# Sparse attention of a two-layer decoder: the compressed keys' weights for both row blocks in one pass, another layout and other PSUM banks for the first products, and a new order of steps

## The chip, the cores and the metric

The kernel runs on one core of one Trainium2 chip. The metric is the device time of one execution in microseconds (us): the median over runs, and for the profile one execution of its own. A core has five engines with a queue each: TensorE (PE, whose weight loads are shown as PEld), VectorE (DVE), ScalarE (ACT), GpSimd (POOL) and SyncE (SP, which here only issues DMAs). An engine takes its instructions in the order of the program; it waits where an operand isn't ready, and what stands behind waits with it.

## What is computed

A trunk of two layers on x of 256 rows by 1024 columns, in float32: each layer is a SwiGLU feed-forward part, a mixer, another feed-forward part, with a layer norm behind each. The second layer's mixer is native sparse attention (NSA), and the change lies in it alone. Cut to what matters:

```python
q, k_c, v_c, k_s, v_s, k_w, v_w, g = split(x @ w_in)     # 16 heads of 64 in 4 groups; 4 key/value heads
q, k_s, k_w = rope(q), rope(k_s), rope(k_w)
gates = sigmoid(g)                                       # three per head
def compress(t, pe, w1, w2):                             # 15 blocks of 32 rows, 16 apart
    blk = concatenate([ch[:, :-1], ch[:, 1:]], axis=2) + pe   # ch: t cut into pieces of 16 rows
    return gelu(blk . w1) @ w2
k_cmp, v_cmp = rope(compress(k_c, ...)), compress(v_c, ...)
p_cmp = masked_softmax(q . k_cmp);  o_cmp = p_cmp . v_cmp
o_slc, o_win = softmax attention with k_s, v_s and with k_w, v_w   # 256 rows: every block is chosen
out = (g0 * o_cmp + g1 * o_slc + g2 * o_win) @ w_out
```

## The kernel before

The 256 rows are two row blocks, T = 0 and 1, of 128 rows, one row per partition. A product with a weight matrix is three matmuls (`mm3`): the weights are cut into a high part `whi` (a rounded copy, ACT, L221) and a low part `wlo` (the rest, DVE, L222), and so are the activations. Weights come in pieces of up to 128x1024 by DMA into four `raw` buffers; a ring of eight split pieces (`RING`) runs ahead of PE, and a piece's place comes free when PE has used it for T = 1. The order in which the weights lie and stream is that of the steps.

`nsa` is written as steps, and the table `ORDER` says in which order they are emitted; the scheduler of the framework then fixes each engine's queue. The letters:

- `c`, `k`, `V`, `Q` (with a row block; `Q` with a group g ahead of it): the products for the compressed branch's keys and values, the other keys, the other values, and a group's four query heads. Each fills one PSUM bank.
- `CV`, `K`, `T`: PE transposes of c, k and q, four to a bank; ACT (and DVE) copy them out. For q there is a chain of engines: DVE (`rope`, L545 and L547), POOL (sum, L550), ACT (high part, L552), POOL (low part, L553), PE (transposes, L718), ACT (L720).
- `B`, `H`, `TK`, `KC`, `HV`: the compression. `B` adds the position table to c (`blk`, DVE, L654) and splits it into `bst` (L306, L307); `H` multiplies `bst` with w1 (L665).
- `C`: for a group and row block, scores against the compressed keys (`kc`), a softmax over 16 columns for 4 heads, and its gate's factor; the result `pc` is split into `pcs`. All of its steps lie on DVE but for the exponential (ACT, L744) and the product with the factor (POOL, L728).
- `S`: scores of a group and row block against k, their maximum (DVE, L772), exponentials (ACT, L775), product with the factor (POOL, L728). `P`: transposes of `pcs`. `A`: transposes of the weights `p` (L784), copies `pt` (L306, L307), products with the values (L796). `F`: the output product of a row block and the layer norm.
- `G`: the gates' sigmoid, an exponential on ACT.

PSUM has eight banks of 128x512: four with the name `o`, two `g`, two `t`. All products c, k, V and Q use the two `g` banks, and transposes the two `t` banks; `o` belongs to the layers' output sums and to S.

## Time and profile before

| | before |
|---|---|
| median of 3 runs | 1104.36 us (1103.11 to 1104.6) |
| the profiled execution: its own time | 1104.31 us |
| its span (first to last instruction) | 1102.5 us |
| PE, DVE, ACT, POOL busy (share of the span) | 97%, 65%, 51%, 7% |
| granted TensorE clock over the span | 0.993 |
| NSA stage | about 742 to 918 us of the span |

The span is what the engines' rows cover; 1.8 us of the execution lie around it. A busy share is an average over six stages; the stage of the change is looked at apart below.

### The profile page before, as it was taken

What the parts mean: (1) busy time and instruction counts of PE and PEld (TensorE: products, weight loads), DVE (VectorE), ACT (ScalarE), POOL (GpSimd) and SP (SyncE); (2) the same over time, 40 slices, a digit from 0 to 9 for tenths busy, and PEclk for the clock granted to TensorE, in tenths of its full rate; (3) what the DMA queues carried; (4) which work ended last, traced back from release to release, by engine and by line L of the source; (5) the groups of instructions that cost most, each with busy time, mean ns of one, the idle gap of its engine ahead of it and who ended that gap; (6) DMA issues with size and microseconds to landing.
All of it is one profiled execution on the core that took longest, in us unless ns stands there. A gap on an engine that the chain in (4) does not pass through costs nothing.

```text
span 1102.5 us, 14514 instructions
## 1 busy us (share of the span) xinstructions
...
## 2 busy tenths in 40 slices
...
GB/s 266 316 209 207 178 156 203 314 195 221 203 215 172 210 160 229 225 195 181 161 199 240 209 196 189 214 168 196 195 204 68 40 38 220 233 215 172 226 157 38
DMA packets 59686, 210.42 MB, mean 191 GB/s; under 512 B 6880, under 2 KB 7264, under 8 KB 58720
## 3 DMA queue, kind: packets, MB, share of 16 engines
...
HBM read 208.43 MB, written 1.05 MB: 190 GB/s over the span
## 4 chain that ended last, share of the span: by engine, by line
PE 84%; DVE 7%; DMA 4%; ACT 2%; issue 2%; POOL 1%; SPq 0%; DVEq 0%; ACTq 0%
PE ps_g L276 17%; PE ps_g L274 17%; PE ps_g L275 17%; PE ps_o L274 9%; PE ps_o L276 9%; PE ps_o L275 9%; DMA raw<-in_w_dram 3%; PE ps_t L313 3%; DVE wlo L222 2%; PE ps_g L796 1%; ACT whi L221 1%; PE ps_t L498 1%; PE ps_o L770 1%; PE ps_t L784 1%; DMA x<-in_w_dram 1%
## 5 line engine op out<-in xcount | busy, mean ns | idle before, releaser
L222 DVE TENSOR_TENSOR wlo<-raw,whi 128x1024 fp32r<-128x1024 f32 (+2 forms) x379 | 454.0, 1204 | 199.6 <-ACT whi L221 190.3
L221 ACT ACTIVATE whi<-raw 128x1024 fp32r<-128x1024 f32 (+2 forms) x379 | 391.9, 1037 | 245.7 <-PE ps_g L276 135.8
L274 PE MATMUL ps_g<-whi,xT0h 128*128 128x512 f32 (+3 forms) x520 | 192.3, 370 | 5.3 <-ACT whi L221 2.8
L274 PE MATMUL ps_g<-whi,xT1h 128*128 128x512 f32 (+3 forms) x520 | 191.9, 369 | 1.5 <-DVE rope L547 1.3
L276 PE MATMUL ps_g<-whi,xT0l 128*128 128x512 f32 (+3 forms) x520 | 191.6, 368 | 0.0
L276 PE MATMUL ps_g<-whi,xT1l 128*128 128x512 f32 (+3 forms) x520 | 191.6, 368 | 0.0
L275 PE MATMUL ps_g<-wlo,xT1h 128*128 128x512 f32 (+3 forms) x520 | 191.5, 368 | 0.0
L275 PE MATMUL ps_g<-wlo,xT0h 128*128 128x512 f32 (+3 forms) x520 | 191.5, 368 | 0.0
L274 PE MATMUL ps_o<-whi,hTh 128*128 128x512 f32 x352 | 137.0, 389 | 0.0
L276 PE MATMUL ps_o<-whi,hTl 128*128 128x512 f32 x352 | 133.4, 379 | 0.0
L275 PE MATMUL ps_o<-wlo,hTh 128*128 128x512 f32 x352 | 133.4, 379 | 0.0
L274 PEld LDWEIGHTS ps_g<-whi,xT0h 128*128 128x128 f32 x520 | 98.8, 190 | 18.8 <-ACT whi L221 5.5
L274 PEld LDWEIGHTS ps_g<-whi,xT1h 128*128 128x128 f32 x520 | 98.8, 190 | 13.2 <-issue 1.9
L275 PEld LDWEIGHTS ps_g<-wlo,xT0h 128*128 128x128 f32 x520 | 98.7, 190 | 11.8 <-DVE wlo L222 0.2
L276 PEld LDWEIGHTS ps_g<-whi,xT1l 128*128 128x128 f32 x520 | 98.9, 190 | 11.6
L275 PEld LDWEIGHTS ps_g<-wlo,xT1h 128*128 128x128 f32 x520 | 98.9, 190 | 11.3
L276 PEld LDWEIGHTS ps_g<-whi,xT0l 128*128 128x128 f32 x520 | 98.8, 190 | 11.3
L363 DVE SCALAR_TENSOR_TENSOR h<-g,ps_g 128x512 f32<-128x512 f32 (+1 forms) x48 | 30.6, 638 | 67.2 <-PE ps_g L276 63.4
L276 PEld LDWEIGHTS ps_o<-whi,hTl 128*128 128x128 f32 x352 | 66.5, 189 | 9.4
L326 POOL TENSOR_TENSOR rstd<-rstd,const 128x1 f32<-128x1 f32 x14 | 13.2, 946 | 916.0 <-DVE rstd L325 916.0
L275 PEld LDWEIGHTS ps_o<-wlo,hTh 128*128 128x128 f32 x352 | 66.7, 189 | 8.3
L274 PEld LDWEIGHTS ps_o<-whi,hTh 128*128 128x128 f32 x352 | 66.6, 189 | 8.3
...
## 6 DMA issues: line engine op xcount, KB each, us to landing
...
```

What stands on the lines that cost most here:

```text
L221: nc.scalar.activation(hi[:, c:e], t[:, off + c:off + e], AF.Copy)
L222: nc.vector.tensor_tensor(lo[:, c:e], t[:, off + c:off + e], hi[:, c:e].bitcast(F32), ALU.subtract)
L274: nc.tensor.matmul(o, a[0], b[0], start=first, stop=False)
L275: nc.tensor.matmul(o, a[0], b[1], start=False, stop=False)
L276: nc.tensor.matmul(o, a[1], b[0], start=False, stop=last)
L313: nc.tensor.transpose(t[:, i * P:(i + 1) * P], src[:, i * P:(i + 1) * P], ident)
L326: nc.gpsimd.tensor_tensor(r, r, const[:, C_EXP:C_EXP + 1], ALU.pow)
L363: nc.vector.scalar_tensor_tensor(h, g, 0.5, u, ALU.mult, ALU.mult)
L498: nc.tensor.matmul(t[:, sl[i]], ws[:, 2 * c + i, :], n[:, sl[i]], start=True, stop=True)
L770: nc.tensor.matmul(o[:, i], qT[:, h0 + h + i, :], kT[k][:, g, :, :w], start=k == 0, stop=False)
L784: nc.tensor.transpose(t[:, i * P:(i + 1) * P], x, ident)
L796: nc.tensor.matmul(pv[:, :n], v.rearrange("p a b -> p (a b)"), x[:, c:c + n], start=first, stop=last and x is pt[-1])
```

## The change

- `compressed` (C) takes both row blocks of a group in one pass over 8 heads: eight score matmuls into one bank, the softmax steps on tiles twice as wide and half as many. Its product with the factor goes from POOL to DVE, and the rounded copy of `pcs` from DVE to ACT (`split`). `pcs` is now one tile per group for both row blocks, two in turn.
- `gate` works on both row blocks at once.
- c is stored by place in the half block: `cT` is ordered (place m of 8, key head g, half block n), written by an ACT copy that reads PSUM in steps of 16 columns and takes only the rows that its 64 partitions need. `blk` then reads runs of 15 columns that lie side by side, and has two buffers.
- The products c and k of T = 1 and both V use `o` banks.
- `ORDER` changes: both Q of group 0 ahead of H0; both V ahead of TK and H1; K1 and KC later; one C for two; A200 ahead of S212, T31 and C3 ahead of P1, A210 later. With it the weights' order changes: group 0's q ahead of w1 of the keys, v ahead of w1 of the values.

The diff, with twelve columns of indentation cut:

```diff
...
 ORDER = """
-    c0 CV0 k0 c1 k1 CV1 B0 H0 B1 Q00 Q01 TK T00 K1 V0 H1 KC K0 V1 T01 G C00 S000 HV Q10 S010 C01 T10 |
-    Q11 P0 S012 A000 T11 P1 Q20 A010 C10 C11 S100 T20 A012 S110 P0 Q21 S112 A100 T21 Q30 P1 A112 S200
-    C20 A110 T30 Q31 P0 S210 C21 A200 C30 S212 P1 S300 A210 T31 C31 P0 A300 F0 S312 A212 S310 P1 A312
+    c0 CV0 k0 c1 k1 CV1 B0 Q00 Q01 H0 B1 T00 K0 V0 V1 TK H1 T01 K1 KC G C0 S000 HV Q10 S010 T10 |
+    Q11 P0 S012 A000 T11 P1 Q20 A010 C1 S100 T20 A012 S110 P0 Q21 S112 A100 T21 Q30 P1 A112 S200
+    C2 A110 T30 Q31 P0 S210 A200 S212 T31 C3 P1 S300 A210 P0 A300 F0 S312 A212 S310 P1 A312
     A310 F1
...
 kc = pool.tile([P, NKV, 2, 16], F32R, name="kc", tag="kc")
-gates = [pool.tile([P, NH, 3], F32, name=f"gate{T}", tag=f"gate{T}") for T in (0, 1)]
+gates = pool.tile([P, 2, NH, 3], F32, name="gate", tag="gate")
 got = {}
...
     if g == 0:
-        nc.vector.tensor_copy(gates[T].rearrange("p a b -> p (a b)"), t[:, :48])
+        nc.vector.tensor_copy(gates[:, T].rearrange("p a b -> p (a b)"), t[:, :48])
     q = pool.tile([P, 4, 2, HD], F32R, name="q", tag="q", bufs=2)
...
 
-    for T in (0, 1):
-        f = gates[T].rearrange("p a b -> p (a b)")
-        nc.scalar.activation(f, f, AF.Exp, scale=-1.0)
-        nc.vector.tensor_scalar(f, f, 3e38, 1.0, ALU.min, ALU.add)
-        nc.vector.reciprocal(f, f)
-        if T == 0:
-            nc.vector.tensor_scalar(gates[T][:, :, 0], gates[T][:, :, 0], const[:, C_ANY:C_ANY + 1], None, ALU.mult)
+    f = gates.rearrange("p t a b -> p (t a b)")
+    nc.scalar.activation(f, f, AF.Exp, scale=-1.0)
+    nc.vector.tensor_scalar(f, f, 3e38, 1.0, ALU.min, ALU.add)
+    nc.vector.reciprocal(f, f)
+    nc.vector.tensor_scalar(gates[:, 0, :, 0], gates[:, 0, :, 0], const[:, C_ANY:C_ANY + 1], None, ALU.mult)
 
...
 nc.sync.dma_start(pe.rearrange("p a b -> p (a b)"), ins["pe"])
-cT = [pa.tile([P, NKV, S + 2], F32, name=f"cT{i}", tag=f"cT{i}") for i in (0, 1)]
+cT = [pa.tile([P, 8, NKV, 16], F32, name=f"cT{i}", tag=f"cT{i}") for i in (0, 1)]
 n60 = NKV * NCMP
...
     turn[T](xT)
-    t = psum("g")
+    t = psum("o" if T else "g")
     gemm_in(t, xT[T], pl["c"], T == 1)
-    c = pa.tile([P, 8, 2, HD], F32, name="c", tag="c", bufs=2)
+    c = pa.tile([P, 8, 2, HD], F32, name="c", tag="ck", bufs=3)
     nc.scalar.activation(c, twice(t, 8), AF.Copy)
...
 def k_step(T):
-    t = psum("g")
+    t = psum("o" if T else "g")
     gemm_in(t, xT[T], pl["k"], T == 1)
-    k2 = pa.tile([P, 8, 2, HD], F32, name="k2", tag="k2", bufs=2)
+    k2 = pa.tile([P, 8, 2, HD], F32, name="k2", tag="ck", bufs=3)
     for b in (0, 1):
...
 def turn_cv(T):
+
     for i in (0, 1):
-        t = turn4(got["c", T], i)
-        nc.scalar.activation(cT[i][:64, :, 1 + T * P:1 + T * P + P], t[:64], AF.Copy)
-        nc.scalar.activation(cT[i][64:, :, T * P:T * P + P], t[64:], AF.Copy)
+        t = turn4(got["c", T], i).rearrange("p g (n m o) -> p o m g n", m=8, o=2)
+        for o in (0, 1):
+            r = slice(64 * o, 64 * o + 64)
+            nc.scalar.activation(cT[i][r, :, :, 8 * T:8 * T + 8], t[r, o], AF.Copy)
 
...
 def v_step(T):
-    t = psum("g")
+    t = psum("o")
     gemm_in(t, xT[T], pl["v"], T == 1)
...
 def cmp_block(i):
-    sv = cT[i][:, :, 1:1 + 256].rearrange("p g (n l) -> p g n l", l=16)
     for m0 in (0, 8):
-        blk = pa.tile([P, 8, n60], F32, name="blk", tag="blk")
-        s = sv[:, :, (m0 // 8):(m0 // 8) + NCMP, 0:16:2].rearrange("p g n m -> p m g n")
+        blk = pa.tile([P, 8, n60], F32, name="blk", tag="blk", bufs=2)
+        s = cT[i][:, :, :, m0 // 8:m0 // 8 + NCMP]
         nc.vector.tensor_tensor(
...
 pb = oT = None
-pcs = [pool.tile([P, 4, 48], F32R, name=f"pcs{T}", tag=f"pcs{T}") for T in (0, 1)]
-for T in (0, 1):
-    nc.gpsimd.memset(pcs[T].bitcast(U32), 0)
+pcs = [pool.tile([P, 2, 4, 48], F32R, name=f"pcs{i}", tag=f"pcs{i}") for i in (0, 1)]
+for i in (0, 1):
+    nc.gpsimd.memset(pcs[i].bitcast(U32), 0)
+turned = [0, 0]
 
...
 
-def scaled(p, sm, gate):
-
+def factor(sm, gate):
     f = small.tile(list(sm.shape), F32, name="f", tag="f")
...
     nc.vector.tensor_tensor(f, f, gate, ALU.mult)
-    nc.gpsimd.tensor_tensor(p, p, f[..., None].to_broadcast(list(p.shape)), ALU.mult)
+    return f
 
-def compressed(g, T):
+def compressed(g):
 
-    qT = got["qT", g, T]
     o = psum("t")
-    for h in range(4):
-        nc.tensor.matmul(o[:, 32 * h:32 * h + 32], qT[:, h, :], kc[:, g].rearrange("p a b -> p (a b)"),
-                         start=True, stop=True)
-    p = pool.tile([P, 4, 16], F32, name="pc", tag="pc", bufs=2)
-    m = small.tile([P, 4], F32, name="mc", tag="mc")
-    nc.vector.tensor_reduce(p, o[:, :128].rearrange("p (h i n) -> p h n i", h=4, i=2), AX.X, ALU.add)
-    mask = const[:, C_MASK + 16 * T:C_MASK + 16 * T + 16]
-    nc.vector.tensor_tensor(p, p, mask[:, None, :].to_broadcast([P, 4, 16]), ALU.add)
+    for T in (0, 1):
+        for h in range(4):
+            c = P * T + 32 * h
+            nc.tensor.matmul(o[:, c:c + 32], got["qT", g, T][:, h, :], kc[:, g].rearrange("p a b -> p (a b)"),
+                             start=True, stop=True)
+    all8 = [P, 8, 16]
+    pc = pool.tile([P, 2, 4, 16], F32, name="pc", tag="pc", bufs=2)
+    p = pc.rearrange("p t h n -> p (t h) n")
+    m = small.tile([P, 8], F32, name="mc", tag="mc")
+    nc.vector.tensor_reduce(p, o[:, :256].rearrange("p (h i n) -> p h n i", h=8, i=2), AX.X, ALU.add)
+    mask = const[:, C_MASK:C_MASK + 32].rearrange("p (t n) -> p t n", n=16)
+    nc.vector.tensor_tensor(pc, pc, mask[:, :, None, :].to_broadcast([P, 2, 4, 16]), ALU.add)
     nc.vector.tensor_reduce(m, p, AX.X, ALU.max)
-    nc.vector.tensor_tensor(p, p, m[:, :, None].to_broadcast([P, 4, 16]), ALU.subtract)
+    nc.vector.tensor_tensor(p, p, m[:, :, None].to_broadcast(all8), ALU.subtract)
     nc.scalar.activation(p, p, AF.Exp)
-    nc.vector.tensor_reduce(m, p, AX.X, ALU.add)
-    scaled(p, m, gates[T][:, 4 * g:4 * g + 4, 0])
-    hi, lo = pcs[T][:, :, 0:16], pcs[T][:, :, 32:48]
-    nc.vector.tensor_copy(hi, p)
-    nc.vector.tensor_tensor(lo, p, hi.bitcast(F32), ALU.subtract)
+    m4 = small.tile([P, 2, 4], F32, name="mc4", tag="mc4")
+    nc.vector.tensor_reduce(m4.rearrange("p t h -> p (t h)"), p, AX.X, ALU.add)
+    f = factor(m4, gates[:, :, 4 * g:4 * g + 4, 0])
+    nc.vector.tensor_tensor(pc, pc, f[..., None].to_broadcast([P, 2, 4, 16]), ALU.mult)
+    c = pcs[g % 2].rearrange("p t h c -> p (t h) c")
+    split(c[:, :, 0:16], c[:, :, 32:48], p)
 
 def turn_c(T):
+    c = pcs[turned[T] % 2]
+    turned[T] += 1
     t = psum("t")
     for h in range(4):
-        nc.tensor.transpose(t[:48, h * P:(h + 1) * P], pcs[T][:, h, :].bitcast(F32), ident)
+        nc.tensor.transpose(t[:48, h * P:(h + 1) * P], c[:, T, h, :].bitcast(F32), ident)
     pct = pb.tile([P, 512], F32R, name="pct", tag="pct", bufs=2)
...
                                      accum_out=sm[:, h + i, r:r + 1])
-    scaled(p, sm, gates[T][:, 4 * g + h0:4 * g + h0 + nh, 1:3])
+    f = factor(sm, gates[:, T, 4 * g + h0:4 * g + h0 + nh, 1:3])
+    nc.gpsimd.tensor_tensor(p, p, f[..., None].to_broadcast(list(p.shape)), ALU.mult)
     got["p", g, T, h0] = p
```

What that does to the queues, at three places. DVE, from the last pieces of c and k's weights on (`wlo` of 912 and 608 columns is group 0's q, the others of 1024 w1 and v); first before:

```order
L222 TENSOR_TENSOR wlo<-raw,whi 128x912 x2
L222 TENSOR_TENSOR wlo<-raw,whi 128x608
L545 TENSOR_TENSOR rope_6586<-ps_g,const 128x4x32 x2
L547 TENSOR_TENSOR rope_6587<-ps_g,const 128x256
L545 TENSOR_TENSOR rope_6592<-ps_g,const 128x4x32 x2
L654 TENSOR_TENSOR blk<-cT_6367,pe 128x480
L547 TENSOR_TENSOR rope_6593<-ps_g,const 128x256
L222 TENSOR_TENSOR wlo<-raw,whi 128x1024
L307 TENSOR_TENSOR bst<-blk,bst 128x8x60
L584 COPY gate_6354<-ps_g 128x48
L654 TENSOR_TENSOR blk<-cT_6367,pe 128x480
```

and now:

```order
L223 TENSOR_TENSOR wlo<-raw,whi 128x912 x2
L223 TENSOR_TENSOR wlo<-raw,whi 128x608
L223 TENSOR_TENSOR wlo<-raw,whi 128x1024 x3
L546 TENSOR_TENSOR rope_6585<-ps_o,const 128x4x32 x2
L548 TENSOR_TENSOR rope_6586<-ps_o,const 128x256
L546 TENSOR_TENSOR rope_6591<-ps_o,const 128x4x32 x2
L654 TENSOR_TENSOR blk<-cT_6366,pe 128x480
L548 TENSOR_TENSOR rope_6592<-ps_o,const 128x256
L654 TENSOR_TENSOR blk<-cT_6366,pe 128x480
L223 TENSOR_TENSOR wlo<-raw,whi 128x1024
L308 TENSOR_TENSOR bst<-blk,bst 128x8x60 x2
```

The three pieces of q's weights come first and one piece of w1 has moved behind the rope of k; both halves of `blk` stand together, and the rope of k reads an `o` bank.

PE, at the transposes of q of group 1, T = 0 (the last `ident,q` here), which stand within the product Q11 (`xT1`, 256 columns); before:

```order
L274 MATMUL ps_g<-whi,xT1h 128x256
L275 MATMUL ps_g<-wlo,xT1h 128x256
L276 MATMUL ps_g<-whi,xT1l 128x256
L274 MATMUL ps_g<-whi,xT1h 128x256
L275 MATMUL ps_g<-wlo,xT1h 128x256
L276 MATMUL ps_g<-whi,xT1l 128x256
L274 MATMUL ps_g<-whi,xT1h 128x256
L718 MATMUL ps_t<-ident,q 128x128 x4
L275 MATMUL ps_g<-wlo,xT1h 128x256
L276 MATMUL ps_g<-whi,xT1l 128x256
L274 MATMUL ps_g<-whi,xT1h 128x256
L275 MATMUL ps_g<-wlo,xT1h 128x256
```

and now:

```order
L776 MATMUL ps_o<-kTl,qT 128x512
L777 MATMUL ps_o<-maskr,identr 128x2x128
L275 MATMUL ps_g<-whi,xT1h 128x256
L276 MATMUL ps_g<-wlo,xT1h 128x256
L277 MATMUL ps_g<-whi,xT1l 128x256
L275 MATMUL ps_g<-whi,xT1h 128x256
L276 MATMUL ps_g<-wlo,xT1h 128x256
L277 MATMUL ps_g<-whi,xT1l 128x256
L275 MATMUL ps_g<-whi,xT1h 128x256
L276 MATMUL ps_g<-wlo,xT1h 128x256
L706 MATMUL ps_t<-w_6362,hv 48x64 x8
L719 MATMUL ps_t<-ident,q 128x128 x4
```

Before, 19 of Q11's 24 matmuls stand ahead of these transposes, now 8.

DVE, behind the rope of the same q (the row ahead of these); before:

```order
L726 RECIPROCAL f<-mc 128x4
L772 TENSOR_REDUCE nm<-ps_o 128x2
L727 TENSOR_TENSOR f<-f,gate_6354 128x4
L772 TENSOR_REDUCE nm<-ps_o 128x2
L748 CAST pcs_6374<-pc 128x4x16
L739 TENSOR_REDUCE pc<-ps_t 128x64
L749 TENSOR_TENSOR pcs_6374<-pc,pcs_6374 128x4x16
L726 RECIPROCAL f<-sm 128x8
L307 TENSOR_TENSOR vcmp<-ps_t,vcmp 48x4x64
L727 TENSOR_TENSOR f<-f,gate_6354 128x8
L741 TENSOR_TENSOR pc<-pc,const 128x64
L222 TENSOR_TENSOR wlo<-raw,whi 128x1024
```

and now:

```order
L742 TENSOR_REDUCE pc<-ps_t 128x128
L679 COPY hv<-ps_t 128x8x15
L744 TENSOR_TENSOR pc<-pc,const 128x128
L679 COPY hv<-ps_t 128x8x15
L745 TENSOR_REDUCE mc<-pc 128x8
L778 TENSOR_REDUCE nm<-ps_o 128x2
L746 TENSOR_TENSOR pc<-pc,mc 128x128
L778 TENSOR_REDUCE nm<-ps_o 128x2
L223 TENSOR_TENSOR wlo<-raw,whi 128x1024
L749 TENSOR_REDUCE mc_6995<-pc 128x8
L308 TENSOR_TENSOR vcmp<-ps_t,vcmp 48x4x64
L726 RECIPROCAL f<-mc_6995 128x8
```

The two row blocks' steps, which stood apart, are one row each of 128 columns (`pc`) for two of 64; the cast is gone from DVE.

## Rows read from the trace of the kernel before

**Rows 1.** Windows of the NSA stage: stretch, length, busy PE PEld DVE ACT POOL, clock, DMA.
```profile
742.00:780.00 38.00, 37.66 (x190) 32.06 (x189) 31.46 (x44) 22.53 (x28) 6.68 (x8) 1.00 0.60 194
780.00:819.00 39.00, 34.47 (x246) 30.51 (x245) 37.45 (x67) 33.38 (x52) 9.88 (x8) 1.00 0.60 205
819.00:830.00 11.00, 8.64 (x54) 7.80 (x52) 8.18 (x24) 7.61 (x26) 9.62 (x7) 0.84 0.56 185
830.00:918.00 88.00, 83.08 (x529) 69.86 (x528) 77.68 (x190) 62.70 (x188) 31.50 (x27) 1.00 0.17 53
```
**Rows 2.** PE in order of time: matmuls behind an idle stretch (length, releaser).
```profile
783.52 0.37 PE L274 MATMUL ps_g<-whi,xT1h 128*128 128x304 f32 x1 [1.25 <-DVE rope L547]
786.29 0.35 PE L665 MATMUL ps_t<-whi,bst 128*128 128x256 f32 x1 [1.50 <-DVE gate L584]
...
824.75 1.11 PE L718 MATMUL ps_t<-ident,q 128*128 128x128 f32 x4 [2.36 <-POOL q L553]
...
849.72 0.50 PE L796 MATMUL ps_g<-pt,vv 128*128 128x256 f32 x2 [1.11 <-DVE pt L307]
...
885.29 0.62 PE L796 MATMUL ps_g<-pt,vv 128*128 128x256 f32 x3 [1.20 <-DVE pt L307]
```

**Rows 3.** DVE in order of time: both ends of the stretch without a pause.
```profile
780.11 0.48 DVE L545 TENSOR_TENSOR rope<-ps_g,const 128x128 f32<-128x128 f32 x2
...
818.43 0.41 DVE L547 TENSOR_TENSOR rope<-ps_g,const 128x256 f32<-128x256 f32 x1
```

**Rows 4.** POOL and DVE in order of time, around the wait at 824.75.
```profile
821.33 3.36 POOL L553 TENSOR_TENSOR q<-rope,q 128x256 fp32r<-128x256 f32 x1 [0.86 <-ACT q L552]
821.60 1.21 DVE L222 TENSOR_TENSOR wlo<-raw,whi 128x1024 fp32r<-128x1024 f32 x1
...
832.86 0.73 POOL L553 TENSOR_TENSOR q<-rope,q 128x256 fp32r<-128x256 f32 x1 [2.33 <-ACT q L552]
```

**Rows 5.** The three us behind that wait, columns as in rows 1.
```profile
825.00:828.00 3.00, 3.00 (x14) 2.73 (x14) 2.23 (x7) 0.86 (x3) 3.00 (x2) 0.50 0.87 299
```

**Rows 6.** Groups of DVE, 742 to 920: busy us, mean ns, idle before.
```profile
L222 DVE TENSOR_TENSOR wlo<-raw,whi 128x1024 fp32r<-128x1024 f32 (+2 forms) x43 | 53.5, 1257 | 1.8 <-ACT whi L221 1.4
L772 DVE TENSOR_REDUCE nm<-ps_o 128x2 f32<-128x512 f32 (+1 forms) x24 | 16.3, 679 | 0.5 <-PE ps_o L771 0.3
...
L545 DVE TENSOR_TENSOR rope<-ps_g,const 128x128 f32<-128x128 f32 x24 | 5.8, 281 | 1.7 <-PE ps_g L276 1.5
...
L748 DVE CAST pcs<-pc 128x64 fp32r<-128x64 f32 x8 | 5.1, 635 | 2.7 <-POOL pc L728 2.6
L547 DVE TENSOR_TENSOR rope<-ps_g,const 128x256 f32<-128x256 f32 x12 | 4.9, 412 | 1.0 <-POOL k L555 1.0
...
L749 DVE TENSOR_TENSOR pcs<-pc,pcs 128x64 fp32r<-128x64 f32 x8 | 3.1, 386 | 0.0
...
L739 DVE TENSOR_REDUCE pc<-ps_t 128x64 f32<-128x128 f32 x8 | 2.3, 286 | 0.9 <-PE ps_t L735 0.7
L743 DVE TENSOR_TENSOR pc<-pc,mc 128x64 f32<-128x64 f32 x8 | 2.2, 277 | 0.1
...
L741 DVE TENSOR_TENSOR pc<-pc,const 128x64 f32<-128x64 f32 x8 | 1.7, 218 | 0.1
L742 DVE TENSOR_REDUCE mc<-pc 128x4 f32<-128x64 f32 x8 | 1.7, 211 | 0.1
L745 DVE TENSOR_REDUCE mc<-pc 128x4 f32<-128x64 f32 x8 | 1.7, 210 | 0.9 <-ACT pc L744 0.9
```

**Rows 7.** The tile blk: shortest, median and longest ns of who writes and reads it.
```profile
L654 DVE TENSOR_TENSOR blk<-cT,pe x4: 986/1238/1802, 781.2 to 794.1; 128x480 f32<-128x480 f32 x4
...
L307 DVE TENSOR_TENSOR bst<-blk,bst x4: 644/1009/1712, 784.4 to 796.9; 128x480 fp32r<-128x480 f32 x4
```

**Rows 8.** Groups of ACT, 742 to 920, columns as in rows 6.
```profile
L593 ACT ACT_TABLE_LOAD x2 | 2.6, 1283 | 0.0
...
L636 ACT ACTIVATE cT<-ps_t 64x512 f32<-64x512 f32 x4 | 2.4, 594 | 0.0
```

## The prediction

> **What bounds the kernel now.** I read the page first: PE is busy for 97% of the span, so outside the NSA stage there is nothing here to win, and the change touches nothing there. Then the stage in four stretches [rows 1]. PE's idle time is the length less its busy time: 0.34 us in the products of c and k (742 to 780), 4.53 us in the products of q and v with the compression (780 to 819), 2.36 us at one place (819 to 830), 4.92 us in the attention (830 to 918); in all 12.15 us. The kernel's matmuls are the same in number and size before and after, so these 12.15 us, and what the clock costs, are all that can be won.
>
> What ends the idle stretches is read from PE in order of time [rows 2]. The first (1.25 us) is a bank: group 0's q needs a `g` bank that DVE's rope of k hasn't read yet. The second (1.50) is named after DVE's gate copy, but the matmul that waits reads `bst`, which DVE had just finished. So both are DVE. In the second stretch DVE is busy for 37.45 of 39 us: from 780.11, the rope of k, to 818.84, the end of the rope of q for group 1, it hardly stops [rows 1, 3]. That queue sets the pace there. The wait of 2.36 us at 824.75 is that q's chain: its last link, the low part on POOL, took 3.36 us, against 0.73 us for the same instruction at 832.86 [rows 2, 4]. Two DVE weight splits of 1.21 us ran meanwhile, the first at 821.60. Behind that wait the clock stands at 0.50 for three us, the lower of its two levels, 1.2 GHz; the stretch's mean is 0.84, which costs at most 11 x 0.16 = 1.8 us [rows 1, 5]. Waits of 1.25 and 1.50 us, and of 1.11 and 1.20 later, left the mean clock of their stretches at 1.00.
>
> The Trainium skill (SBUF — State Buffer, Who interferes with whom) says that a VectorE instruction with two SBUF inputs and a GpSimd instruction that reads SBUF exclude each other for their whole length. The trace agrees, 3.36 us against 0.73 beside the splits.
>
> **The change, part by part.**
>
> *Compressed weights.* A pass costs DVE now five steps of 286, 218, 211, 277 and 210 ns, a cast of 635 and a low part of 386 [rows 6], together 2.22 us, 17.8 us for eight. Four passes of double width cost, if an instruction's length hardly follows its 64 columns, 1.20 us of steps, 0.39 for the low part and a product with the factor of about 0.28 (as the subtraction): 1.87, 7.5 us for four. If length doubles with the width: 2.40 + 0.77 + 0.55 = 3.72, 14.9 us. So DVE saves 2.9 to 10.3 us; I take 8, nearer to the short end, since the reduction of 512 columns takes 679 ns and the one of 128 takes 286 [rows 6], half of which is no work on columns. The cast goes to ACT as four copies; they lie beside ACT's other work, which fills 62.7 of 88 us [rows 1]. POOL loses eight products; they stand among its `p` products, and PE waits for neither.
>
> *Layout of c.* `blk` reads in steps now: 986 ns undisturbed, against 644 for the low part of the same 128x480 in `bst`, which reads side by side [rows 7]. With runs of 15 a `blk` lies between these two. I take 0.64, four times 0.34, 1.4 us of DVE (bounds 0 and 1.4). The eight ACT copies have half the columns, 256 for 512: 0.30 us each if they go by columns, 0.59 as now if the steps in PSUM cost as much as they save [rows 8]. I take 0.40; it saves ACT 1.5 us and puts `blk` no later.
>
> *Gates in one, table loads.* One exponential for two, and the loads of ACT's tables in the stage go from five to three by the order of its queue: 2 x 1.28 = 2.6 us less on ACT [rows 8]. It isn't the pace setter up to 819, at 33.4 of 39 us, so I count nothing for itself; it is the cover for the copies that move there. The gates are first read in C0, long after both q of group 0, so waiting for the second costs nothing.
>
> *Idle banks.* k of T = 1 is read by DVE's rope late (780.11), and group 0's q no longer needs its bank: the 1.25 us go. The `o` banks used are those that the layer norm of T = 0 read before this stage's products began. One buffer less for c and k costs nothing, since c of T = 0 is turned before k of T = 1 is copied.
>
> *Order.* q's two products (48 matmuls of 304 columns at 2.4 GHz, 6.1 us) now stand between c's transposes and H0, and cover the wait for `bst` (1.50). Their three weight pieces stream ahead of w1's, whose last DMA lands about as much later, beside q's products. V is emitted whole ahead of TK and H1, which covers the gelu and copy between H0 and its two small products. SP's queue holds the same pieces, and the load of the layer norm's weights stays behind four of them.
>
> **The sum.** First the DVE queue up to the rope of group 1's q, now at 818.84. Ahead of it stand one weight piece more (group 3's second; +1.26), no steps of C (-1.20), two copies of `hv` less (about the reduction's 0.29 each, -0.6) and cheaper `blk` (-1.4): 816.9. Bounds: 815.4 if DVE's 1.55 us of pauses close as well, 818.3 if `blk` gains nothing. Then POOL 0.73, ACT about 0.4, POOL 0.73 and three handovers of about 0.1 [rows 4]: the transposes of q start at 819.1, for 824.75 now. Since 11 matmuls of Q11 (256 columns, 1.2 us) now come behind them, the same work stands at 820.3: **4.4 us** won (1.8 if the splits block POOL again by 2.63; 6.0 with the pauses closed).
>
> The clock's **1.8 us** come back if that wait is short; PE is ready for these transposes at about 817, so a wait of about 2 us remains. Rows show no fall behind 1.50 and one behind 2.36, so I take back a third: **-0.6**.
>
> Next is late what stands behind in DVE's queue: the low part of `pcs`, for `turn_c`. Between the rope and it stand two splits (2.51), two maxima (1.36), another rope (0.97) [rows 6], C0's other steps (2.2 of those above) and small rows of about 0.15 to 0.4 (1.8): 8.8 us, 825.7. PE has S012, S100 and the rest of Q11 ahead of it, some 4.4 us of columns, and would be there at 823.7: **-2.0** (0 to -3).
>
> In the attention two waits of 1.11 and 1.20 us end with `pt` on DVE [rows 2]; both copies stood behind a cast or low part of `pcs`, and the cast is gone and DVE has 8 us less: **+2.3** (0 to 4.9). The reshuffled A, S and T may open waits that no row shows; between 0 and the 1.20 of the longest now I take **-0.8**.
>
> Together 4.4 + 1.8 - 0.6 - 2.0 + 2.3 - 0.8 = 5.1 us. The profiled execution took 1104.31 us, its span and 1.8 around it, level with the median of 1104.36; so 1104.3 - 5.1 = **1099.2 us**.
>
> **Rivals.**
>
> *The pace stays with POOL and DVE.* The low part of q on POOL is blocked again (1.8 us won in place of 4.4), the clock falls again (nothing back), and PE, arriving late, doesn't wait for `turn_c`; the attention wins 0.3 since its waits move elsewhere. 1104.3 - 2.1 = 1102.2. For it: more splits now stand in DVE's queue ahead. Against it: the next split stands eight rows behind the rope.
>
> *Slower: one chain for two.* `turn_c` of T = 0 now needs T = 1's scores too, and C's steps with two SBUF inputs (mask, maximum, factor, low part: four in a row) stand against POOL's `p` products. The cast's mean of 635 ns, over twice that of a step of the same width [rows 6], shows what such a block does. If each of the four chains costs PE 2.5 us, 10 us are lost, of which the 5.1 won pay half, and the clock falls once more behind one of them (0.6): 1104.3 + 5.5 = 1109.8. It decides from 5.1 / 4 = 1.3 us a group. Against it: DVE's saving, and 5.2 to 6.9 us of PE columns between scores and transposes in each group.
>
> *Reading PSUM in steps is dear.* If the stepped copies of c cost by the ratio of `blk`'s rows, 986 / 644, on today's length, one takes 0.91 us; four lie between c's last transposes and the queue that needs them, 1.3 us more than now. The start of `blk` slips by it and DVE idles: 1099.2 + 1.3 = 1100.5. The Trainium skill (SBUF — State Buffer, Door 1: The DMA port swizzle) says that PSUM has lines of 8 bytes and that a step across them is penalized; `blk`'s rows agree for SBUF, none shows it for ACT and PSUM.
>
> **How the numbers follow.** The forecast has 0.62, the dear copies 0.12, the pace that stays 0.16, slower 0.10. A measurement of this kernel can tell 0.2%, 2.2 us, from no change. The first two are faster (0.74), the third lies on the edge of no change (0.16), the last is slower. The range: the best ends give 6.0 + 1.8 + 4.9 - 3.0 = 9.7, so 1094.6; the third case reaches to 1102.2 and, with nothing won in the attention and a `turn_c` wait of 2.0, 1104.5. I take 1094.5 to 1104.0, which leaves out the slower case and edges.
>
> **What would show it.** The stretch up to T10's transposes shorter by some 4 us, no wait ahead of group 0's q or of H0; POOL's low part near 0.7 us; `blk` near 0.65 us and C's wide steps near 0.3; a wait of one to two us at the first `turn_c`; no PE wait that ends with `pt` behind `pcs`. It is wrong if DVE still fills the stretch to 819, if the weights of v or w1 arrive after PE asks for them, or if new waits above 1.3 us a group stand ahead of `turn_c`.

## The result, and the profile after

The changed kernel is slower: 1115.53 us, median of 4 runs (1112.43 to 1116.35), beside 1104.48 for the kernel before in the same session; ratio 1.0092 (1.0071 to 1.0114). The forecast was 1099.2 with a range up to 1104.0. The profiled execution took 1112.43 us, its span is 1110.7 (1102.5 before). Lines of the changed kernel carry numbers up to eight higher: L308 is the low part of a split, L554 q's low part on POOL, L784 the product of p on POOL, L760 the transposes of `pcs`.

Windows of the changed kernel, columns as in [rows 1]; the last three lie within the stretches above them:

```profile
742.00:780.00 38.00, 36.16 (x185) 30.91 (x183) 30.07 (x43) 21.02 (x27) 6.90 (x8) 1.00 0.59 191
780.00:819.00 39.00, 34.07 (x219) 30.48 (x218) 35.54 (x55) 28.99 (x45) 12.11 (x7) 0.91 0.66 209
819.00:830.00 11.00, 9.66 (x82) 8.81 (x80) 10.05 (x28) 9.50 (x31) 4.24 (x4) 1.00 0.50 159
830.00:918.00 88.00, 79.69 (x488) 65.74 (x489) 71.38 (x151) 57.83 (x178) 29.39 (x22) 0.96 0.14 40
794.00:802.00 8.00, 6.75 (x23) 5.72 (x24) 7.61 (x12) 7.56 (x12) 1.06 (x1) 0.57 0.66 197
...
830.00:838.00 8.00, 6.69 (x40) 5.80 (x41) 7.24 (x11) 5.18 (x20) 4.58 (x4) 0.79 0.38 105
...
853.00:861.00 8.00, 6.07 (x34) 5.16 (x35) 7.27 (x13) 4.24 (x13) 3.52 (x4) 0.79 0.34 78
```

PE's idle time is now 1.84, 4.93, 1.34 and 8.31 us, in all 16.4 for 12.15 in [rows 1]. The clock stood at 0.91 over 39 us and 0.96 over 88, where before it was 0.84 over 11: 7.0 us of lost columns for 1.8. Together 9.5 us, near the 8.2 by which the span grew (half a hundredth of the clock is 0.6 us over 127).

Where it is lost shows in the matmul columns that PE has done by a time; their sum is the same in both traces. The changed kernel reached as many as the kernel before had 1.5 us earlier at 742 and 2.2 us earlier at 830, and then 3.0 us later at 834, 5.9 at 853, 7.3 at 877 and 8.4 at 935. So up to 830 gains and losses cancel, and the loss lies in the attention.

PE in order of time, the places that the prediction spoke of and the new long wait:

```profile
791.28 0.66 PE L719 MATMUL ps_t<-ident,q 128*128 128x128 f32 x4 [0.91 <-POOL q L554]
...
795.25 1.97 PE L628 MATMUL ps_t<-ident,k 128*128 128x128 f32 x8 [2.66 <-DVE ch L670]
...
823.63 0.66 PE L719 MATMUL ps_t<-ident,q 128*128 128x128 f32 x4
...
831.31 0.82 PE L760 MATMUL ps_t<-ident,pcs 128*48 128x128 f32 x4 [2.65 <-DVE pcs L308]
...
854.93 0.60 PE L760 MATMUL ps_t<-ident,pcs 128*48 128x128 f32 x4 [2.80 <-DVE pcs L308]
...
893.09 0.60 PE L760 MATMUL ps_t<-ident,pcs 128*48 128x128 f32 x4 [1.06 <-DVE pcs L308]
```

The transposes of T10 (823.63) wait for nothing, where the forecast had left about 2 us; the 2.36 us of [rows 2] are gone. But 2.66 us stand ahead of the transposes of k at 795.25, where nothing was forecast, and the four waits for `pcs` are 2.65, 2.80, 0.29 and 1.06, 6.8 us for a forecast of 2.0, which was made for the first of them alone. Behind each of the three longest waits shown here the clock fell to its lower level (0.57 over 794 to 802, 0.79 over 830 to 838 and over 853 to 861, mixtures of 1.2 and 2.4 GHz).

DVE and POOL of the changed kernel in order of time, where the low parts of `pcs` are made:

```profile
827.17 1.81 DVE L727 TENSOR_TENSOR f<-f,gate 128x4 f32<-128x4 f32 x1
...
829.43 1.73 DVE L308 TENSOR_TENSOR pcs<-pc,pcs 128x128 fp32r<-128x128 f32 x1
...
850.77 2.12 DVE L223 TENSOR_TENSOR wlo<-raw,whi 128x1024 fp32r<-128x1024 f32 x1 [0.34 <-ACT whi L222]
852.81 1.98 DVE L308 TENSOR_TENSOR pcs<-pc,pcs 128x128 fp32r<-128x128 f32 x1
...
876.81 0.29 DVE L308 TENSOR_TENSOR pcs<-pc,pcs 128x128 fp32r<-128x128 f32 x1
...
891.25 1.70 DVE L308 TENSOR_TENSOR pcs<-pc,pcs 128x128 fp32r<-128x128 f32 x1
```

```profile
821.82 0.74 POOL L554 TENSOR_TENSOR q<-rope,q 128x256 fp32r<-128x256 f32 x1 [0.80 <-ACT q L553]
827.06 1.90 POOL L784 TENSOR_TENSOR p<-p,f 128x1024 f32<-128x1024 f32 x1 [4.50 <-DVE f L726]
829.12 1.89 POOL L784 TENSOR_TENSOR p<-p,f 128x1024 f32<-128x1024 f32 x1 [0.16 <-DVE f L727]
...
849.91 4.73 POOL L784 TENSOR_TENSOR p<-p,f 128x1024 f32<-128x1024 f32 x2 [8.47 <-ACT sv L815]
...
870.36 1.90 POOL L784 TENSOR_TENSOR p<-p,f 128x1024 f32<-128x1024 f32 x1 [4.08 <-ACT pt L307]
878.21 0.73 POOL L551 TENSOR_TENSOR rope<-rope,rope 128x256 f32<-128x256 f32 x1 [5.95 <-DVE rope L548]
...
890.90 1.90 POOL L784 TENSOR_TENSOR p<-p,f 128x1024 f32<-128x1024 f32 x1 [3.23 <-DVE f L727]
```

The low part of `pcs` is 0.29 us long where POOL is idle (876.81, between products that ended at 872.3 and began at 878.2), and 1.70 to 1.98 us where POOL multiplies `p`; it ends when that product ends (829.43 + 1.73 = 831.16, 829.12 + 1.89 = 831.01). The 512 numbers of `f` took 1.81 us for the same reason, and two of POOL's products took 4.73 us where a weight split stood against them. The Trainium skill's rule that the prediction named (SBUF — State Buffer, Who interferes with whom) is seen here in both directions.

ACT of the changed kernel, ahead of the wait at 795.25:

```profile
789.35 1.99 ACT L222 ACTIVATE whi<-raw 128x1024 fp32r<-128x1024 f32 x2
791.35 1.28 ACT L593 ACT_TABLE_LOAD   x1
...
793.43 0.42 ACT L553 ACTIVATE q<-rope 128x256 fp32r<-128x256 f32 x1 [0.50 <-POOL rope L551]
...
794.37 0.38 ACT L669 ACTIVATE ch<-ps_t 60x256 f32<-60x256 f32 x1
...
795.40 0.60 ACT L721 ACTIVATE qT<-ps_t 128x512 fp32r<-128x512 f32 x1
```

Both transpose banks wait for ACT. One is freed by `ch` (the compression's sums before the gelu, copied out of PSUM), whose ACT copy (794.37) stands behind two weight copies, a table load, q's high part (which waited for POOL) and a `bst`; the other by `qT` (795.40). PE had finished H0 at 790.4.

### The profile page after: what moved, and what is told of

Read it like the earlier page. It is cut to its first block, busy times and chain, and to the rows that moved or that the text cites. A ratio compares the mean times of both kernels' runs of the same rounds, so it can differ in the third digit from the quotient of the medians.

```text
span 1110.7 us, 14456 instructions
## 1 busy us (share of the span) xinstructions
PE 1077.6 (97%) x5437; PEld 942.2 (85%) x5437; DVE 721.1 (65%) x933; ACT 558.6 (50%) x795; POOL 68.8 (6%) x61
## 4 chain that ended last, share of the span: by engine, by line
PE 83%; DVE 8%; DMA 3%; ACT 2%; issue 2%; POOL 1%; SPq 0%; DVEq 0%; ACTq 0%
PE ps_g L277 16%; PE ps_g L275 16%; PE ps_g L276 16%; PE ps_o L275 9%; PE ps_o L276 9%; PE ps_o L277 9%; DMA raw<-in_w_dram 3%; PE ps_t L314 3%; DVE wlo L223 3%; ACT whi L222 1%; PE ps_g L803 1%; PE ps_t L499 1%; PE ps_t L791 1%; DVE x L344 1%; PE ps_o L776 1%
## 5 line engine op out<-in xcount | busy, mean ns | idle before, releaser
L223 DVE TENSOR_TENSOR wlo<-raw,whi 128x1024 fp32r<-128x1024 f32 (+1 forms) x379 | 456.0, 1210 | 200.5 <-ACT whi L222 191.0
L222 ACT ACTIVATE whi<-raw 128x1024 fp32r<-128x1024 f32 (+1 forms) x379 | 392.0, 1037 | 249.7 <-PE ps_g L277 133.6
L275 PE MATMUL ps_g<-whi,xT0h 128*128 128x512 f32 (+3 forms) x512 | 189.1, 369 | 4.0 <-ACT whi L222 1.9
L277 PE MATMUL ps_g<-whi,xT0l 128*128 128x512 f32 (+3 forms) x512 | 188.5, 368 | 0.0
L275 PE MATMUL ps_g<-whi,xT1h 128*128 128x512 f32 (+3 forms) x496 | 182.4, 368 | 0.0
L277 PE MATMUL ps_g<-whi,xT1l 128*128 128x512 f32 (+3 forms) x496 | 181.7, 367 | 0.0
L276 PE MATMUL ps_g<-wlo,xT1h 128*128 128x512 f32 (+3 forms) x496 | 181.7, 366 | 0.0
L275 PEld LDWEIGHTS ps_g<-whi,xT1h 128*128 128x128 f32 x496 | 94.0, 190 | 10.9 <-ACT xT1h L307 0.2
L277 PEld LDWEIGHTS ps_g<-whi,xT1l 128*128 128x128 f32 x496 | 93.9, 189 | 10.8
L276 PEld LDWEIGHTS ps_g<-wlo,xT1h 128*128 128x128 f32 x496 | 94.0, 189 | 10.6
```

The lines of the kernel that those rows point to most:

```text
L222: nc.scalar.activation(hi[:, c:e], t[:, off + c:off + e], AF.Copy)
L223: nc.vector.tensor_tensor(lo[:, c:e], t[:, off + c:off + e], hi[:, c:e].bitcast(F32), ALU.subtract)
L275: nc.tensor.matmul(o, a[0], b[0], start=first, stop=False)
L276: nc.tensor.matmul(o, a[0], b[1], start=False, stop=False)
L277: nc.tensor.matmul(o, a[1], b[0], start=False, stop=last)
```

## The experiments

Medians in us; beside them the ratio to the kernel before (whose median was 1103.8 to 1104.6 in these sessions) with its 95% interval.

| run | what differs | median | ratio |
|---|---|---|---|
| e1 | changed kernel, K0 behind V0 | 1116.1 | 1.010 (1.0084 to 1.0115) |
| e2 | changed, POOL's product of p in four | 1112.1 | 1.0062 (1.0044 to 1.0081) |
| e3 | changed, no low part of `pcs` | 1108.7 | 1.0033 (1.0023 to 1.0043) |
| e4 | changed, two passes | 1110.8 | 1.0055 (1.004 to 1.007) |
| e5 | changed, old table, one pass | 1114.6 | 1.008 (1.005 to 1.011) |
| e6 | changed, old table, two passes | 1111.2 | 1.0057 (1.0035 to 1.0079) |
| e7 | e6 with the product of p in four | 1118.0 | 1.0115 (1.0092 to 1.0138) |
| e8 | changed, product of p on DVE | 1106.9 | 1.0016 (1.0001 to 1.0032) |
| e9 | before, idle banks alone | 1104.7 | 1.0008 (0.9997 to 1.002) |
| e10 | before, layout of c alone | 1112.8 | 1.009 (1.0061 to 1.0119) |
| e11 | before, merged gates alone | 1109.1 | 1.0048 (1.0029 to 1.0067) |
| e12 | before, product of p on DVE | 1105.5 | 1.0007 (0.9996 to 1.0019) |
| e13 | before, LATER 160 | 1114.7 | 1.009 (1.0061 to 1.0118) |
| e14 | before, LATER 150 | 1112.9 | 1.0085 (1.0052 to 1.0117) |
| e15 | changed, LATER 125 | 1109.3 | 1.0044 (1.0028 to 1.0061) |
| e16 | e6 with the product of p on DVE | 1108.9 | 1.0036 (1.0018 to 1.0053) |
| e17 | e8 with LATER 150 | 1105.1 | 1.0009 (0.9997 to 1.0021) |
| e18 | e8, q's sum and low part on DVE too | 1110.9 | 1.0059 (1.0047 to 1.0072) |

No version beats the kernel before. Most of these edits also give the queues another order: beside the changed kernel some 80, 200 and 290 of PE's 5437 rows stand elsewhere in the traces of e3, e2 and e8, and 120 in e15, where nothing but the order differs. So a difference between two runs is in general that of an edit and an order together; e9 (no other order) and e7 (nearly that of e6) are the exceptions.

**e1, the wait at k.**

```diff
- ... B0 Q00 Q01 H0 B1 T00 K0 V0 V1 TK H1 ...
+ ... B0 Q00 Q01 H0 B1 T00 V0 K0 V1 TK H1 ...
```

> Edit: in the table of steps K0 (transposes of k, T = 0) stands behind V0. Theory: the changed kernel lost its time at two kinds of place. One is the wait of 2.66 us ahead of the eight transposes of k at 795.25, with the clock at 0.57 over the next 8 us (3.4 us of columns); both transpose banks were held there by copies on ScalarE that came late. The other is the four waits ahead of the transposes of pcs (6.8 us). If the first is a matter of place, 24 matmuls of V0 (5.2 us) cover the copies: no wait above 1 us there, clock 1.00 over 794 to 802, and the time falls by 3 to 6 us, to 1109.5 to 1112.5 (VectorE has 3 us of slack in 802 to 819, so not all need come back); the waits at pcs stay. Rival: the engines that split V's weights set the pace there, and PE only waits for a low part of V's third piece instead: the time stays within 1114 to 1117.

1116.1: the rival held. What PE waited for from 742 to 935 (us in total, times, longest):

```profile
PE ps_t L760 <- DVE pcs L308: 6.9, 4, 2.8
PE ps_t L689 <- DVE hk L679: 2.4, 1, 2.4
...
PE ps_o L276 <- DVE wlo L223: 1.5, 1, 1.5
PE ps_o L776 <- ACT qT L721: 1.2, 1, 1.2
```

The 2.66 us are gone, and 1.5 at a low part of V's weights, 2.4 at `hk` and 1.2 at `qT` have come. ACT and DVE were busy for 7.92 and 7.61 of the 8 us from 794, so they seem to set the pace there: moving K0 only moved PE's waits.

**e2 and e3, the low part of `pcs`.**

```diff
-nc.gpsimd.tensor_tensor(p, p, f[..., None].to_broadcast(list(p.shape)), ALU.mult)
+for j in range(0, 2 * nh, n):            # n = 256 // w, p8 and f8 with (h r) as one axis
+    nc.gpsimd.tensor_tensor(p8[:, j:j + n], p8[:, j:j + n], f8[:, j:j + n, None].to_broadcast([P, n, w]), ALU.mult)
```

> Edit: GpSimd's product of p with its factor is cut into four instructions of 256 columns each. Theory: the low part of pcs on VectorE took 1.73 and 1.98 us because GpSimd's products of 1.9 to 2.4 us held it up, and so did the small product f before it (1.81). With pieces of about 0.5 us no VectorE instruction of two SBUF inputs is held longer than about 0.6 us: low parts of pcs at 0.3 to 0.9 us, the four waits at pcs fall from 6.8 to 2 to 4 us, and one of the two falls of the clock behind them goes: 1108 to 1112. The wait at the transposes of k stays. Rival: the rows that stand ahead in VectorE's queue (weight splits, rope) make it late, not the holding up: the waits at pcs stay above 5 us and the time within 1114 to 1117.

```diff
-split(c[:, :, 0:16], c[:, :, 32:48], p)
+nc.scalar.activation(c[:, :, 0:16], p, AF.Copy)
```

> Edit: the low part of pcs is left out (its columns keep the zeros of the start), so the compressed weights are used rounded only; the rest is as in the changed kernel. Theory: with it gone the transposes of pcs wait only for ScalarE's high part, which stood 3.5 us (group 0) and 3.9 us (group 1) ahead of the low part: no wait above 0.8 us at pcs, clock 1.00 there, time down by the 6.8 us of waits and 2 to 3 us of clock: 1105 to 1108. Rival, one chain for two row blocks is late as such (scores of T = 1, softmax steps, the high part): the waits at pcs stay above 4 us in sum and the time above 1111.

The low parts of `pcs` in e2 (shortest, median and longest ns, first and last start):

```profile
L308 DVE TENSOR_TENSOR pcs<-pc,pcs x4: 277/345/614, 829.7 to 893.2; 128x128 fp32r<-128x128 f32 x4
```

It was 289, 1712 and 1975 ns in the changed kernel. So the holding up is shown, and the waits at `pcs` fell to 0.3 us. The time fell by 3.5 us only, to the edge of what was expected: a piece takes 744 ns in the mean (612 at the median), so POOL's products cost 34.2 us for 23.7, and a wait of 3.8 us for `pt` on ACT opened at 839.95. e3 gives 6.8 us back, a little less than expected; its waits at `pcs` are gone too, and 3.4 us for `pt` and 1.9 for the rope have come.

**e4 to e6, a square of two orders by one or two passes.** e4 has before's `compressed` on the changed kernel's tiles, and from its second line on before's table; e5 has before's table with one C a group, e6 both, so that the order tested is that of the table's first line. Undone in e4 and e6:

```diff
-def compressed(g):
+def compressed(g, T):
...
-    f = factor(m4, gates[:, :, 4 * g:4 * g + 4, 0])
-    nc.vector.tensor_tensor(pc, pc, f[..., None].to_broadcast([P, 2, 4, 16]), ALU.mult)
...
-    split(c[:, :, 0:16], c[:, :, 32:48], p)
+    scaled(p, m, gates[:, T, 4 * g:4 * g + 4, 0])
...
+    nc.vector.tensor_copy(hi, p)
+    nc.vector.tensor_tensor(lo, p, hi.bitcast(F32), ALU.subtract)
```

The table's first line in e5 (in e6 C00, and C01 ahead of T10):

```diff
-    c0 CV0 k0 c1 k1 CV1 B0 Q00 Q01 H0 B1 T00 K0 V0 V1 TK H1 T01 K1 KC G C0 S000 HV Q10 S010 T10 |
+    c0 CV0 k0 c1 k1 CV1 B0 H0 B1 Q00 Q01 TK T00 K1 V0 H1 KC K0 V1 T01 G C0 S000 HV Q10 S010 T10 |
```

> Edit: only the compressed weights are undone: one pass for each row block, product with the factor on GpSimd, high part on VectorE, steps C in the places of the kernel before; the layout of c, banks, merged gates and the order up to the attention stay changed. Theory: the first pass needs T = 0 only and is ready early, so the waits at pcs go back to what they were (none above 0.3 us), and the time falls by 6 to 10 us though VectorE has some 8 us more to do: 1105 to 1110; what is left against the kernel before is the wait at the transposes of k with its clock. Rival: the order ahead of the attention is what costs, and the one pass is worth its VectorE time: the time stays at 1113 or above.

> Edit: the changed kernel with the table of steps of the kernel before, C once a group at the place of its second pass's neighbour (C0 after G, C1 after A010, C2 after S200, C3 after T31); one pass, layout of c, banks and gates stay changed. With the run that undid the one pass (1110.8 against 1115.5) and the next run it makes a square of two orders by one or two passes. Theory: one pass costs about 4.7 us through the low part of pcs whatever the order ahead of it, and the new order costs about as much again: 1106 to 1110, with waits at pcs of 4 us or more in sum. Rival: one pass is dear only where the new order puts it: then this run lies within 2 us of the next one.

> Edit: one pass and the table of steps are both undone; what stays of the change is the layout of c, the idle banks and the merged gates. Theory: these parts do no harm; they take away the wait of 1.25 us on a bank at 783.5 and some 1.4 us of VectorE in blk: 1102 to 1105, that is 0 to 2.5 us faster than before, and the wait of 2.66 us at the transposes of k (with its low clock) is gone, since those stand behind H0, both q and the first half of V as before. Rival: the idle banks or the stepped copies are what moves the waits: the time stays at 1108 or above.

With one pass the kernel is 4.7 us slower in the new order and 3.4 in the old one; the new order by itself costs nothing that can be told (1110.8 against 1111.2, 1115.5 against 1114.6). e4 lies between its two ranges, e5 outside both. The surprise is the corner where both are undone: layout, banks and gates, which should have won up to 2.5 us, are 7 us slower than before. In e5 the waits at `pcs` are 0.3 us, against my theory: none of its low parts is held up (273 to 295 ns), though the products of p are on POOL. It waits 5.6 us for `pt` on ACT in their place. And in e6, with two passes, the waits at `pcs` are 3.4 us (3.8 in e10, 3.3 in e14), with low parts of up to 1.85 us. So they come with an order, not with one pass as such.

**e9 to e11, the three parts one by one**, each on the kernel before:

```diff
-t = psum("g")
+t = psum("o" if T else "g")
...
```

> Edit: the kernel before with nothing changed but the banks: c and k of T = 1 and both V in the idle banks. Every engine's queue is the same as before (only the bank's name changes in its rows). The kernel with layout, banks and gates of the change but two passes and the old table took 1111.2, 7 us more than before, and waited 3.68 us at the first product of bst. Theory A, the banks cost it: the wait of 1.25 us at 783.5 goes, PE spends its q products earlier and then waits as much longer for bst, and low clock follows: 1107 or above. Theory B, the banks are harmless and it is the order that layout and gates bring about: 1102.5 to 1105, the 1.25 us moved to bst (2.7 in place of 1.50) or won.

```diff
-nc.scalar.activation(cT[i][:64, :, 1 + T * P:1 + T * P + P], t[:64], AF.Copy)
-nc.scalar.activation(cT[i][64:, :, T * P:T * P + P], t[64:], AF.Copy)
+nc.scalar.activation(cT[i][r, :, :, 8 * T:8 * T + 8], t[r, o], AF.Copy)
...
```

> Edit: the kernel before with nothing changed but the layout of c (copies in steps of 16, blk from runs of 15 with two buffers). Less work: ScalarE some 1.5 us, VectorE some 1.4 us. But the scheduler of the framework, which sees other lengths, arranges the queues anew: 323 rows of PE's, 205 of VectorE's and 121 of ScalarE's differ beyond line numbers, most of them in the attention. Theory B: it is this new arrangement, not the work, that costs the changed kernel what the two orders and the one pass don't explain: 1106 to 1112, with waits in the attention (a copy pt behind a blocked row of ScalarE, or pcs) that the kernel before doesn't have. Rival, the layout's own work decides: 1101 to 1104.

```diff
-for T in (0, 1):
-    f = gates[T].rearrange("p a b -> p (a b)")
-    nc.scalar.activation(f, f, AF.Exp, scale=-1.0)
+f = gates.rearrange("p t a b -> p (t a b)")
+nc.scalar.activation(f, f, AF.Exp, scale=-1.0)
...
```

> Edit: the kernel before with nothing changed but the gates merged, one exponential for two. Work falls by one table load and a few small rows, nothing else; the arrangement of the queues changes in 349 rows of PE's, 287 of VectorE's and 145 of ScalarE's. As the run before it asks for the price of a new arrangement by itself. Theory B: 1106 to 1112. Rival, only work and waits named in the prediction count: 1102 to 1105.

The banks do nothing to the time (1104.7): the 1.25 us on a bank are gone, but a wait of 1.55 at the transposes of c has come, and the one ahead of H0 has grown from 1.50 to 3.19. The other two cost 8.5 and 4.8 us, though both lessen the work: in e10 `blk` takes 640, 647 and 1568 ns (986, 1238 and 1802 in [rows 7]) and a copy of c 376 ns for the 594 of [rows 8]. PE in e10, in order of time:

```profile
785.11 0.35 PE L666 MATMUL ps_t<-whi,bst 128*128 128x256 f32 x1 [3.53 <-DVE bst L307]
...
834.53 0.50 PE L797 MATMUL ps_g<-pt,vv 128*128 128x512 f32 x1 [3.00 <-ACT pt L306]
```

ACT in e10 ahead of that wait of 3.00 us, then POOL, then DVE:

```profile
831.75 0.42 ACT L552 ACTIVATE q<-rope 128x256 fp32r<-128x256 f32 x1 [3.16 <-POOL rope L550]
...
833.87 1.09 ACT L306 ACTIVATE pt<-ps_t 128x512 fp32r<-128x512 f32 x2
```

```profile
828.12 1.94 POOL L729 TENSOR_TENSOR p<-p,f 128x1024 f32<-128x1024 f32 x1 [1.84 <-DVE f L728]
830.02 1.70 POOL L550 TENSOR_TENSOR rope<-rope,rope 128x256 f32<-128x256 f32 x1
832.25 1.14 POOL L553 TENSOR_TENSOR q<-rope,q 128x256 fp32r<-128x256 f32 x1 [0.53 <-ACT q L552]
```

```profile
829.88 1.26 DVE L222 TENSOR_TENSOR wlo<-raw,whi 128x1024 fp32r<-128x1024 f32 x1
...
831.15 1.66 DVE L222 TENSOR_TENSOR wlo<-raw,whi 128x1024 fp32r<-128x1024 f32 x1
```

Two transposed blocks of `p` lie in PSUM, and ACT's copies of them (`pt`, 833.87) stand behind q's high part in ACT's queue. That one waits 3.16 us for the rope's sum on POOL, which stands behind a product of p and takes 1.70 us for 0.72 because DVE splits weights against it. e11 and e6 show the same wait, 3.01 us at 834.15 and 834.51, with the same 3.16 us on ACT. In the kernel before ACT takes that high part at 832.37 too, but the first two `pt` stand ahead of it:

```profile
829.67 0.60 ACT L306 ACTIVATE pt<-ps_t 128x512 fp32r<-128x512 f32 x1 [0.26 <-PE ps_t L784]
830.93 0.60 ACT L306 ACTIVATE pt<-ps_t 128x512 fp32r<-128x512 f32 x1 [0.66 <-PE ps_t L784]
...
832.37 0.41 ACT L552 ACTIVATE q<-rope 128x256 fp32r<-128x256 f32 x1
```

So an edit that has nothing to do with these rows, the gates' exponential, let the scheduler place one of them ahead of others.

**e13 to e15, the same instructions in another order.** The weights' loads and splits are given a lower priority than the rest by the number LATER.

```diff
-LATER = 130
+LATER = 160        # e13; 150 in e14; both on the kernel before
+LATER = 125        # e15, on the changed kernel
```

> Edit: in the kernel before one number, the priority at which the weights' loads and splits are put behind the other work (LATER), from 130 to 160. The instructions are the same in kind and number; their order differs in 214 rows of PE's queue, 138 of VectorE's and 80 of ScalarE's, in the attention above all. Theory B, the arrangement by itself is worth several us and that of the kernel before is a good one: 1106 to 1112, with waits in 820 to 900 that the kernel before doesn't have. Rival, only work and named waits count and a neutral edit does nothing: 1103 to 1105.5.

> Edit: the same number at 150: 235, 145 and 78 rows differ. A second sample of the same question. Theory B: 1106 to 1112. Rival: 1103 to 1105.5.

> Edit: in the changed kernel the same number, from 130 to 125: 138 rows of PE's queue, 97 of VectorE's and 61 of ScalarE's differ, all of them behind the first groups' scores; the instructions are the same. Theory B: the time moves by 2 us or more from 1115.5, either way, since the waits at pcs move with the arrangement; more likely down, as the changed kernel's is a poor one: 1108 to 1114. Rival, the one pass and the other parts cost what they cost in any arrangement: 1114 to 1117.

Theory B holds, and by more than I gave it: 10.6 and 8.8 us slower, 6.2 us faster, with no instruction added or taken. What PE waited for in e13:

```profile
PE ps_g L796 <- DVE pt L307: 5.1, 6, 1.5
PE ps_t L629 <- DVE ch L670: 2.3, 1, 2.3
PE ps_g L796 <- ACT pt L306: 1.9, 1, 1.9
```

Of the first three waits, 9.3 us together, the kernel before has only 2.7 us at DVE's `pt`. And in e15:

```profile
PE ps_t L628 <- DVE ch L670: 2.7, 1, 2.7
PE ps_g L803 <- ACT pt L307: 2.2, 1, 2.2
...
PE ps_t L760 <- DVE pcs L308: 0.6, 1, 0.6
```

The waits at `pcs`, 6.8 us in the changed kernel, are 0.6 us here with the same one pass: where they open is a matter of the order.

**e7, e8, e12, e16 to e18, POOL and DVE apart.** In e8, e12, e16 and e17 the 12 products of p are on DVE, in e18 q's sum and low part too; e7 cuts them as e2 does. (In e12 and e16 the line sits in a helper that also serves `pc`, whose product stays on POOL.)

```diff
-nc.gpsimd.tensor_tensor(p, p, f[..., None].to_broadcast(list(p.shape)), ALU.mult)
+nc.vector.tensor_tensor(p, p, f[..., None].to_broadcast(list(p.shape)), ALU.mult)   # e8, e12, e16, e17, e18
-nc.gpsimd.tensor_tensor(b, a, b, ALU.add)       # and the low part of q
+nc.vector.tensor_tensor(b, a, b, ALU.add)       # e18
```

> Edit: as the run before, and GpSimd's product of p with its factor in four instructions of 256 columns. Theory of the holding up: in the kernel before too GpSimd's products hold VectorE's small steps and the casts of pcs (mean 635 ns); cut in pieces they give VectorE time back, but the transposes of p wait for the last piece, which ends no earlier: within 2 us of the run before, 1101 to 1106. If GpSimd's fixed cost of an instruction is large, the pieces cost it up to 6 us in all and the transposes of p come late: 1107 or above.

> Edit: in the changed kernel the product of p with its factor goes from GpSimd to VectorE, 12 instructions. Theory of the holding up: nothing on GpSimd is then in VectorE's way in the attention but the sums and low parts of q; the low parts of pcs take 0.3 us each, but the products add some 12 times 1.2 = 14 us to VectorE's queue, which had 14.6 us of pauses in 861 to 930 and 1 to 3 in the stretches before. The waits at pcs fall below 4 us and others open at p: 1108 to 1114. Rival, VectorE's queue as such sets the pace of the attention: 14 us more in it make it slower than the changed kernel, 1117 to 1125.

> Edit: the kernel before, with the 12 products of p with their factor on VectorE in place of GpSimd. In the changed kernel this was worth 8.6 us (1106.9 against 1115.5) though VectorE has some 14 us more to do. Theory: what holds VectorE and GpSimd up against each other costs the kernel before too (the low part of q took 3.36 us for 0.73, the casts of pcs 635 ns), but its queues are arranged so that PE waits little in the attention: 1100 to 1105. If VectorE's queue sets the pace of the attention there (9.1 us of pauses in 861 to 930, 0.6 to 0.9 in the stretches of 8 us before), 1106 to 1112.

> Edit: layout, banks and gates of the change with the old table and two passes (1111.2), and the 12 products of p on VectorE in place of GpSimd. Theory: the arrangement costs because GpSimd's products and VectorE hold each other up where the scheduler counts on neither; with the products off GpSimd the wait of 3.0 us at 834 goes and the time falls to 1102 to 1106, as the changed kernel fell by 8.6 us. Rival, the arrangement costs in other ways too (banks, queues' heads): the time stays at 1108 or above.

> Edit: the run with the products of p on VectorE (1106.9) with the priority of the weights at 150 for 130: the same instructions, 131 rows of PE's queue, 72 of VectorE's and 45 of ScalarE's in another order. Theory: without the holding up an arrangement does what the scheduler counts on, so the time stays within 2.5 us of that run, 1104.5 to 1109.5. Rival, an arrangement is worth several us for other reasons (queues' heads, banks): 1111 or above, or below 1103.

> Edit: as the run with the products of p on VectorE, and q's sum and its low part on VectorE too (16 instructions of 256 columns); GpSimd keeps the sums of k alone. VectorE gets 16 times some 0.42 = 6.7 us more, of which 4 to 5 lie in or near the stretch up to 819 where it sets the pace; in return no rope, weight split or blk is held up by q (a blk of 1.1 us above its least, two splits of 0.5), ScalarE's high part of q comes 0.7 to 1.3 us earlier and with it the copies behind it on which the transposes of k wait. Theory: the wait at the transposes of k falls below 1.5 us and the time lies at 1103 to 1107. Rival, VectorE's queue sets the pace there: 1108 or above.

The low parts of `pcs` in e8, columns as for e2:

```profile
L308 DVE TENSOR_TENSOR pcs<-pc,pcs x4: 282/284/286, 828.7 to 889.7; 128x128 fp32r<-128x128 f32 x4
```

e8 wins 8.6 us with 15.6 us more on DVE, better than expected; there all four low parts are short, and the waits at `pcs` are 0.3 us. In the kernel before the same edit changes nothing that can be told (e12), though the casts of `pcs` take 189 ns there for the 635 of [rows 6]. e16 falls by 2.3 us only: its wait at 834 is gone, as expected, but 3.5 us at `bst` stay and 2.3 at exponentials on ACT have come, so the rival holds for the time. e17 moves by 1.8 us with another order, within what I gave. The four kernels with p on DVE lie at 1105.1 to 1108.9, those with p whole on POOL at 1104.5 to 1116.1; they differ in other parts too, so this is a hint and no proof. e7 is the slowest of all, with nearly the order of e6, so the 6.8 us between them are the price of the pieces: 746 ns each in the mean, and a wait of 4.4 us for `pt`. e18:

```profile
PE ps_t L760 <- DVE pcs L308: 5.0, 4, 3.6
...
PE ps_t L628 <- DVE ch L670: 1.5, 1, 1.5
```

The wait at k falls to 1.5 us, and DVE's longer queue opens 5.0 us at `pcs`: the rival held, and to take q off POOL as well is too much.

## Why the prediction was wrong

*The step that failed* is the last one of the sum: "The reshuffled A, S and T may open waits that no row shows; between 0 and the 1.20 of the longest now I take -0.8." The scheduler arranged the queues anew for nearly every edit here. Two other orders of the kernel before, with the same instructions, are 8.8 and 10.6 us slower (e13, e14), and another order of the changed kernel is 6.2 us faster (e15). So of the 11 us by which the changed kernel is slower than before some 6 hang on its order; how the rest divides stays open. The new table's first line isn't what brings it (e4 to e6). I bounded what can be lost by the waits that the trace of the kernel before shows, but that trace shows one arrangement, a good one. All terms of the sum, 5.1 us, are smaller than what the arrangement can do. That layout and gates cost by the arrangement alone is shown for the size (e13, e14), for the gates by their having less work, and for the common wait at 834 by its rows; that the layout's own work costs nothing at all in e10 is argued from its shorter rows.

*The term for `turn_c`*, -2.0, priced the first group alone. That wait was 2.65, within the bounds given; the other three, put at nothing, were 4.2, and the clock fell twice. I counted 8.8 us of rows in DVE's queue with short lengths, and left to a rival that POOL's products hold them up. With `f` at 0.16 and the low part at 0.29 us, their lengths where no product stands against them, the first low part would have ended at 828.1, an estimate from these rows, and PE came at 828.7: so that wait is the holding up. The rival, one chain for two at 2.5 us a group, named the right mechanism (1.70 to 1.98 us for 0.29); it cost 2.65, 2.80, 0.29 and 1.06. Its sign, new waits above 1.3 us a group, came true. I gave it 0.10, and its sum counts the first group twice: the 5.1 us are net of 2.0 for it, so 2.5 us a group give 1107.8, not 1109.8. (The range's low end, too, takes `turn_c` at its worst, -3.0, among the best ends of the other terms; nothing hangs on it here.) The kernels with one pass are 3.4 to 4.7 us slower (e4 to e6), but not by one pass as such: in e5, e8 and e15 its waits are 0.3, 0.3 and 0.6 us.

*DVE's saving.* Eight us were to go with the compressed weights; C's rows on DVE fell from 17.8 to 14.5 us. Two of its groups in the changed kernel, 742 to 935, columns as in [rows 6]:

```profile
L308 DVE TENSOR_TENSOR pcs<-pc,pcs 128x128 fp32r<-128x128 f32 x4 | 5.7, 1422 | 0.0
...
L744 DVE TENSOR_TENSOR pc<-pc,const 128x128 f32<-128x128 f32 x4 | 2.6, 644 | 0.1
```

The lengths themselves were rightly guessed: in e8, with p off POOL, the two take 284 and 275 ns and all of C's rows 8.4 us. The other 6 us are the holding up.

*The 2.3 us at `pt`* were 1.2: the waits for DVE's `pt` fell from 2.7 to 0.8 us, and one of 0.7 for ACT's came.

*Order.* "V is emitted whole ahead of TK and H1, which covers the gelu" held (the waits of 0.8 us at `hk` and 0.6 at `ch` are gone), but it looked at the wrong place: K0 stands ahead of V0 in the table, and PE's queue has three matmuls of V0 ahead of the transposes of k. The 2.66 us there weren't seen. They cost little by themselves: e1 moved them and lost as much elsewhere, and by 830 the time was made up.

*The 4.4 us of T10.* POOL's low part took 0.74 us, as forecast, and the wait went whole. But DVE ended the rope of that q at 820.2, not 816.9, since PE ended the product of that q only at 819.4, and PE came to the transposes at 823.6 through the waits and the slow clock ahead: counted in columns 0.7 us was won from 742 to 830, no more. *The clock's 1.8 us* became 7.0 lost.

*The costs of operations* were right where nothing holds them up: `blk` 639 ns at its shortest (0.64 forecast), a copy of c 378 (0.40), C's wide steps 0.28 to 0.43. The rival of dear copies fell: ACT takes 378 ns for 256 columns out of PSUM in steps of 16, and 379 for the 256 of `ch` that lie side by side. The penalty that the prediction cited for it (the Trainium skill, SBUF — State Buffer, Door 1: The DMA port swizzle) isn't seen for ACT here; what the Trainium skill says of PSUM there is about matmuls. *The idle banks* did what was said, and the 1.25 us were spent elsewhere (e9).
